# Attention with negated, scaled queries and undivided probabilities, the row sums divided out of a head pair's output

## The chip, the cores and the metric

One Trainium2 chip, one of its NeuronCores. A core has TensorE (PE in the profile, with its weight loads as PEld), VectorE (DVE), ScalarE (ACT), GpSimd (POOL) and SyncE (SP, which here issues nearly all DMAs). Each engine works through its own instructions in order and waits on semaphores for the others. The metric is the device time of one execution in microseconds (us).

## The reference, cut to what matters

The program is one layer of an encoder, applied to two sequences of 512 rows. Beside a recurrent branch (RWKV7, run forwards and backwards) and a feed-forward part it has an attention branch with 8 heads. The change touches this part alone:

```python
sc = (jnp.einsum('bqhd,bkhd->bhqk', qn, k_nope)
      + jnp.einsum('bqhd,bkd->bhqk', qr, k_rope))
prob = jax.nn.softmax(sc.astype(jnp.float32) * scale, axis=-1)   # scale = 96 ** -0.5
return jnp.einsum('bhqk,bkhd->bqhd', prob.astype(v.dtype), v)
```

The softmax of a row is exp(scale * (sc - max)) over its own sum. Dividing by the sum may be done on the probabilities, or on the output row that they are multiplied into.

## The kernel before, in words

The front part of the program (up to about 1000 us) is written as six Python generators, which a small driver (`drive`) interleaves by a virtual clock of TensorE time: each piece of matmul work adds its cost to `pe["now"]`, a generator yields the time at which it wants to go on, and the first one in the list that is due runs next. TensorE instructions are pinned to the order that comes out. The generators, in order of precedence: the recurrence's state steps, its post-processing, the merging of its triangular solves, its preparation, a fill thread (projections, then gates, then the whole attention), and the combination of both branches for the first sequence. The other engines' instructions are placed by a scheduler that simulates the timeline. Constants such as `PL`, `YQ`, `YK` and `YA1` are the virtual times by which the fill thread puts off a step so that its operands may be ready.

Attention goes over 2 sequences, 8 heads and 4 blocks of 128 queries: 64 blocks. For one block:

- `sc`: three fp32r matmuls (high and low parts of queries and keys) of 128x512 into one PSUM bank.
- DVE takes the row maximum into `mx[:, 0:1]` (L605) and multiplies it by -QSCALE (L606).
- ACT computes exp(QSCALE * sc + bias) into `pr` and accumulates the row sum (L608); reading the accumulator is an instruction of its own.
- DVE takes the reciprocal of the sum (L609) and multiplies `pr` by it (L610).
- TensorE transposes `pr` in four pieces into `pt` (L129), and ACT copies `pt` to `pT` (L554). A block waits in the list `pending` until two others stand behind it (`ALAG = 2`), and until `PL` after its scores.

After the fourth block of a pair's second head, `pav` multiplies `pT` of both heads by the values, the even head into partitions 0 to 63 and the odd one into 64 to 127, with queries along the free dimension. DVE copies `pav` to `ob` (L566), which a DMA stores to `o_d`. Queries of the next head come from `attn_q`: six matmuls into `qps`, a multiplication by the rotary table into `qf` on DVE (L539), then a split in high and low parts.

PSUM tiles of the attention (`sc`, `pt`, `pav`, `qps`, `kps`, `vps`) and of the post-processing share four banks (tag "f"), a tile taking the one that comes free; `pr` and `ob` share three buffers in SBUF.

During the attention the recurrence of the last sequences' heads runs in the same stretch (`s`, `o`, `gx`, `gy`, `zp`, `xp` on PE; `rs`, `svb`, `kra`, `bt`, `kt`, `c` on DVE). Towards its end the combination begins: `ld`, `yo` and `pab` on L1032 to L1058, whose loads of `y_d` follow the last post-processing; `pwo` follows at about 1009 us.

Of the kernel before, what the change touches and what calls it, by code (L numbers as in the profile page):

```python
# [10 lines left out]
F32 = mybir.dt.float32  # L11
F32R = mybir.dt.float32r
AF = mybir.ActivationFunctionType
ALU = mybir.AluOpType
AX = mybir.AxisListType
# [3 lines left out]
P = 128  # L19
NB = 2  # L20
S = 512
# [10 lines left out]
QSCALE = 96 ** -0.5  # L32
# [7 lines left out]
ALAG = 2  # L40
# [9 lines left out]
PRE = lambda nc: nc.vector  # L50
# [1 line left out]
NT = 2  # L52
F0 = 10
NE = 2
YA1 = 0.52
YP1 = 7
YP2 = 3
YP3 = 1
# [7 lines left out]
YO2 = 2.11  # L66
YO3 = 3.44
YS = 0.5
YQ = 2.6
YK = 1.4  # L70
OFFS = 200000, 150000, 120000, 100000, 0, 0
JP = NFF // 2
NRH = 10
# [4 lines left out]
HOLDW = 0.7  # L78
PRIOW = 1
C0 = 18  # L80
PL = 3.5
HORD = (0, 1)
VQB = 3
HALVES = (4,)
# [20 lines left out]
def trunk(ctx, tc, outs, x, w_in, w2, g2, w_uq, w_ukk, w_ukv, w_oab, w_out, w_gu, w_down,  # L105
          cols, fng, ident, te, to, mask2, reset, blk64, blk2):
    nc = tc.nc
# [10 lines left out]
    def pin(ins, cost):  # L118
        if pe["pin"]:
            tc.keep_in_program_order(ins)  # L120
        pe["cost"] += cost

    def mm(out, lhsT, rhs, start=True, stop=True, **kw):
        n = math.prod(rhs.shape[1:]) * (1 if rhs.dtype == F32R else 4) / 2400
        pin(nc.tensor.matmul(out, lhsT, rhs, start=start, stop=stop, **kw), n if out.shape[0] > 64 else n / 2)  # L125

    def tr4(ps, src):
        for t in range(4):
            pin(nc.tensor.transpose(ps[:, t * P:(t + 1) * P], src(t), idn), P / 1200)  # L129

    def split(hi, lo, src, eng=None):
        nc.scalar.copy(hi, src)  # L132
        (eng or nc.vector).tensor_sub(lo, src, hi)  # L133

    def mm3(out, whi, wlo, xhi, xlo, start=True, stop=True, **kw):
        mm(out, whi, xhi, start=start, stop=False, **kw)
        yield 0
        mm(out, whi, xlo, start=False, stop=False, **kw)
        yield 0
        mm(out, wlo, xhi, start=False, stop=stop, **kw)  # L140
        yield 0
# [25 lines left out]
    o_d = [[dram.tile([P, S], F32, name=f"o_d{b}{p}") for p in range(NPAIR)] for b in range(NB)]  # L167
# [59 lines left out]
    def pf(name):  # L227
        return psf.tile([P, S], F32, tag="f", bufs=NF, name=name)
# [251 lines left out]
    def attn_ld(ap, src, name, rows=P, q=None):  # L480
        t = ap.tile([P, S], F32, tag="pq", bufs=2, name=name)[0:rows]
        (q or nc.sync).dma_start(t, src)
        return t

    def attn_lat(ap, b, i, t=None):

        if t is None:
            t = attn_ld(ap, mla_d[b][:, i], f"pq{b}{i}", q=None if b else nc.scalar)
        r = [ap.tile([P, S], F32R, tag=f"lat{i}{j}", name=f"lat_{b}{i}{j}") for j in range(2)]
        split(*r, t)  # L490
        return r
# [30 lines left out]
    def attn_kt(kt, ps):  # L522
        for e in range(2):
            rows = slice(0, 64) if e == 0 else slice(64, 128)
            nc.scalar.copy(kt[e][0][rows], ps[rows])
            nc.vector.tensor_sub(kt[e][1][rows], ps[rows], kt[e][0][rows])

    def attn_q(ap, b, hd, qn, tab):
        wq = ap.tile([P, 2 * P], F32, tag="wq", bufs=1, name=f"wq{b}{hd}")
        (nc.sync if b or hd else nc.scalar).dma_start(wq, w_uq[hd])  # L530
        wqh = ap.tile([P, 2 * P], F32R, tag="wqh", bufs=2, name=f"wqh{b}{hd}")
        wql = ap.tile([P, 2 * P], F32R, tag="wql", bufs=2, name=f"wql{b}{hd}")
        split(wqh, wql, wq, QLE(nc))
        ps = pf(f"qps{b}{hd}")
        for i in range(2):
            yield from mm3(ps, wqh[:, i * P:(i + 1) * P], wql[:, i * P:(i + 1) * P], qn[i][0], qn[i][1],
                           start=(i == 0), stop=(i == 1))
        qf = ap.tile([P, S], F32, tag="qf", bufs=1, name=f"qf{b}{hd}")
        nc.vector.tensor_mul(qf, ps, tab[hd % 2])  # L539
        qh = ap.tile([P, S], F32R, tag="qh", bufs=2, name=f"qh{b}{hd}")  # L540
        ql = ap.tile([P, S], F32R, tag="ql", bufs=2, name=f"ql{b}{hd}")
        split(qh, ql, qf, QLE(nc))
        return qh, ql, pe["now"] + pe["cost"] + YQ

    def attention(ap, meanwhile):
        pending = []

        def finish():
            b, hd, qb, pr, pT, at = pending.pop(0)
            p = hd // 2  # L550
            yield "at", at
            pt = pf(f"pt{b}{hd}{qb}")
            tr4(pt, lambda t: pr[:, t * P:(t + 1) * P])
            nc.scalar.copy(pT[hd % 2][:, :, qb * P:(qb + 1) * P], pt.rearrange("p (t q) -> p t q", t=4))  # L554
            if qb < 3 or hd % 2 == 0:
                yield 0
                return
            yield YA1
            pav = pf(f"pav{b}{p}")
            for t in range(4):  # L560
                for e in range(2):
                    mm(pav[e * 64:(e + 1) * 64], vt[b][:, t, (2 * p + e) * 64:(2 * p + e + 1) * 64], pT[e][:, t],
                       start=(t == 0), stop=(t == 3))
                    yield 0
            ob = ap.tile([P, S], F32, tag="pr", bufs=ALAG + 1, name=f"ob{b}{p}")
            nc.vector.tensor_copy(ob, pav)  # L566
            nc.sync.dma_start(o_d[b][p], ob)
            if hd == 7:
                done.add(("attn", b))

        vt = [None] * NB
        pT = [ap.tile([P, 4, S], F32, tag="pT", bufs=2, name=f"pT0{i}") for i in range(2)]
        ldq, ldk = attn_ld(ap, mla_d[0][:, 0], "pq00", q=nc.scalar), attn_ld(ap, mla_d[0][:, 2], "pq02", q=nc.scalar)
        kvn, q0 = attn_lat(ap, 0, 2, ldk), attn_lat(ap, 0, 0, ldq)
        kg = attn_k(ap, 0, 0, kvn)
        meanwhile()
        kps = yield from kg
        qn = [q0, attn_lat(ap, 0, 1)]
        kt = attn_kr(ap, 0)
        attn_kt(kt, kps)  # L580
        tab = []
        for e, src in enumerate((te, to)):
            t = ap.tile([P, S], F32, name=f"tab{e}")
            nc.sync.dma_start(t, src)
            tab.append(t)
        q = yield from attn_q(ap, 0, 0, qn, tab)
        wvr = attn_ld(ap, w_ukv, "wv")
        wv = [ap.tile([P, S], F32R, name=f"wv{j}") for j in range(2)]
        split(*wv, wvr)
        heads = [(b, hd) for b in range(NB) for hd in range(8)]  # L590
        for (b, hd), (b1, hd1) in zip(heads, heads[1:] + [(NB, 0)]):
            qh, ql, at = q
            e = hd % 2
            if e == 0 and (b or hd):
                pT = [ap.tile([P, 4, S], F32, tag="pT", bufs=2, name=f"pT{b}{hd + i}") for i in range(2)]
            if hd == 7 and b1 < NB:
                kvn = attn_lat(ap, b1, 2)
                qn = [attn_lat(ap, b1, i) for i in range(2)]
            for qb in range(4):
                qs = slice(qb * P, (qb + 1) * P)  # L600
                yield "at", at
                sc = pf(f"sc{b}{hd}{qb}")
                yield from mm3(sc, qh[:, qs], ql[:, qs], kt[e][0], kt[e][1])
                mx = ap.tile([P, 4], F32, tag="mx", bufs=4, name=f"mx{b}{hd}{qb}")
                nc.vector.reduce_max(mx[:, 0:1], sc, axis=AX.X)  # L605
                nc.vector.tensor_scalar_mul(mx[:, 1:2], mx[:, 0:1], -QSCALE)  # L606
                pr = ap.tile([P, S], F32, tag="pr", bufs=ALAG + 1, name=f"pr{b}{hd}{qb}")
                nc.scalar.activation(pr, sc, AF.Exp, scale=QSCALE, bias=mx[:, 1:2], accum_out=mx[:, 2:3])  # L608
                nc.vector.reciprocal(mx[:, 3:4], mx[:, 2:3])  # L609
                PRE(nc).tensor_scalar(pr, pr, mx[:, 3:4], 0.0, op0=ALU.mult, op1=ALU.add)  # L610
                pending.append((b, hd, qb, pr, pT, pe["now"] + PL))
                if b1 < NB:
                    if qb == 1:
                        q = yield from attn_q(ap, b1, hd1, qn, tab)
                    if qb == 2 and e == 1:
                        kps = yield from attn_k(ap, b1, hd1 // 2, kvn)
                    if qb == 3 and e == 1:
                        if hd1 == 0:
                            kt = attn_kr(ap, b1)
                        attn_kt(kt, kps)  # L620
                        q = (q[0], q[1], max(q[2], pe["now"] + YK))
                while len(pending) > ALAG:
                    yield from finish()
                if hd == 0 and qb == VQB:
                    vt[b] = yield from attn_v(ap, b, kvn, wv)
        while pending:
            yield from finish()
# [1091 lines left out]
```

## Time and profile before

| | before |
|---|---|
| median of 3 runs | 1831.26 us (1829.73 to 1834.43) |
| time of the profiled execution | 1833.27 us |
| its span, first to last instruction | 1831.4 us |
| PE busy | 1725.9 us, 94% |
| DVE busy | 1116.1 us, 61% |
| ACT busy | 771.4 us, 42% |
| POOL busy | 640.4 us, 35% |
| mean granted TensorE clock | 0.979 |

In views that list instructions, a row has the start in us, the duration in us, the engine, the line and the operation; in brackets stands how long the engine was idle before it, and what ended that. In the views of waits a row has the waiting engine and line, what it waited for, and then the total in us, the number of times and the longest. In tables by stretch each engine has its busy time, with the number of its instructions in brackets; PEclk is the granted TensorE clock. The attention's matmuls start at 721 us with the first `sc`, and the last `pav` ends at 966 us.

### The profile page before, as it was taken

How to read it: one execution, taken by the hardware profiler on the slowest of the kernel's cores; microseconds unless marked ns; L12 is line 12 of the kernel's file. 1: busy time of each engine (PE TensorE's matmuls, PEld its weight loads, DVE VectorE, ACT ScalarE, POOL GpSimd, SP SyncE). 2: the span in 40 equal slices, each digit the busy share in tenths (PEclk: the TensorE clock that was granted, in tenths of full speed). 3: DMA queues.
4: the chain of work that ended last, by engine and by line, in shares of the span. 5: the costliest groups of instructions: out<-in, count | busy, mean ns of one | idle time of the engine just before them, and what ended most of it. 6: DMA issues, size and time to landing. Idle time of an engine off the chain costs nothing.

```text
span 1831.4 us, 30995 instructions
## 1 busy us (share of the span) xinstructions
PE 1725.9 (94%) x11676; PEld 1357.8 (74%) x11676; DVE 1116.1 (61%) x1957; ACT 771.4 (42%) x1496; POOL 640.4 (35%) x992
## 2 busy tenths in 40 slices
PE   6999989999999998899989999699999999989997
PEld 6887767777777775565656979578888888868886
DVE  6633555635355455877776556865655556588757
ACT  5434343333344335666663233333333333335445
POOL 3012345363644627161012124853434333200006
PEclk8999989999999998999999999899999999999999
DMA  4354433434333334212067651022222222374442
GB/s 165 121 175 162 124 106 89 119 80 126 106 107 117 84 109 117 60 34 58 28 240 229 194 175 35 24 81 93 97 96 90 93 81 90 100 270 128 131 139 92
DMA packets 185333, 208.97 MB, mean 114 GB/s; under 512 B 102816, under 2 KB 114464, under 8 KB 185184
## 3 DMA queue, kind: packets, MB, share of 16 engines
q1 hardware_dynamic: 184320, 205.48, 35.9%
q8 instruction: 92, 1.51, 0.3%
q10 hardware_dynamic: 720, 0.98, 0.2%
q0 software_dynamic: 144, 0.52, 0.1%
q14 instruction: 57, 0.47, 0.1%
HBM read 147.70 MB, written 59.24 MB: 113 GB/s over the span
## 4 chain that ended last, share of the span: by engine, by line
PE 67%; DVE 10%; DMA 8%; POOL 7%; issue 4%; ACT 3%; SPq 1%; POOLq 0%; DVEq 0%; ACTq 0%
PE pgC L125 10%; PE pgB L125 6%; PE pgA L125 6%; PE pj_gt L125 6%; PE pj_rkv L125 5%; PE dx L125 5%; PE dy L125 3%; POOL el L841 2%; POOL lt L839 2%; PE pab L125 2%; PE s L125 2%; PE pav L125 2%; PE pj_mla L125 2%; DMA wor<-in_w_out 2%; PE gx L125 2%
## 5 line engine op out<-in xcount | busy, mean ns | idle before, releaser
L839 POOL TENSOR_TENSOR lt<-lane,el 128x126 f32<-128x126 f32 (+22 forms) x248 | 95.6, 386 | 40.8 <-DMA lane<-nt_d 22.3
L841 POOL TENSOR_TENSOR el<-el,lt 128x126 f32<-128x126 f32 (+22 forms) x248 | 98.5, 397 | 19.1
L125 PE MATMUL pab<-yo,wab 128*128 128x512 f32 x384 | 94.8, 400 | 8.3 <-ACT yo L132 3.7
L125 PE MATMUL pj_gt<-h_lo,whi_gt 128*128 128x512 f32 x240 | 99.5, 415 | 0.0
L125 PE MATMUL pj_gt<-h_hi,whi_gt 128*128 128x512 f32 x240 | 99.0, 413 | 0.0
L125 PE MATMUL pj_gt<-h_hi,wlo_gt 128*128 128x512 f32 x240 | 98.4, 410 | 0.5 <-DVE wlo_gt L133 0.5
L125 PE MATMUL pwo<-woh,m 128*128 128x256 f32 x512 | 93.6, 283 | 0.0
L125 PEld LDWEIGHTS pab<-yo,wab 128*128 128x128 f32 x384 | 71.0, 190 | 29.1 <-DVE wab L133 4.8
L1209 POOL TENSOR_TENSOR s<-uraw 128x512 f32<-128x512 f32 x22 | 29.2, 1328 | 153.3 <-DMA uraw<-in_w_gu 153.3
L125 PEld LDWEIGHTS pwo<-woh,m 128*128 128x128 f32 x512 | 80.3, 192 | 0.3
L125 PE MATMUL pj_rkv<-h_hi,whi_rkv 128*128 128x512 f32 x192 | 79.4, 414 | 0.0
L125 PE MATMUL pj_rkv<-h_hi,wlo_rkv 128*128 128x512 f32 x192 | 79.0, 415 | 0.0
L125 PE MATMUL pj_rkv<-h_lo,whi_rkv 128*128 128x512 f32 x192 | 78.4, 409 | 0.0
L125 PE MATMUL pwo<-wol,m 128*128 128x256 f32 x256 | 72.4, 284 | 0.5 <-DVE wol L133 0.5
L1588 POOL TENSOR_TENSOR x<-x,dp 128x512 f32<-128x512 f32 x4 | 6.3, 1590 | 176.9 <-DVE x L1587 176.9
L1277 DVE TENSOR_TENSOR p<-p,pgC 128x512 f32<-128x512 f32 x22 | 15.1, 687 | 86.9 <-PE pgC L125 86.9
L1056 POOL TENSOR_TENSOR g<-g 128x512 f32<-128x512 f32 x16 | 24.5, 1533 | 97.1 <-DVE g L1054 85.9
L928 ACT COPY sva<-s 64x128 f32<-64x128 f32 x64 | 16.5, 257 | 95.6 <-PE s L125 86.3
L466 POOL TENSOR_SCALAR lut<-lut 128x512 f32<-128x512 f32 x32 | 20.5, 642 | 98.4 <-ACT lut L464 98.1
L929 DVE COPY svb<-s 64x128 f32<-64x128 f32 x64 | 18.9, 295 | 57.6 <-ACT sva L928 34.8
L125 PEld LDWEIGHTS pj_gt<-h_hi,wlo_gt 128*128 128x128 f32 x240 | 45.1, 188 | 9.4 <-DVE wlo_gt L133 1.2
L125 PEld LDWEIGHTS pj_gt<-h_hi,whi_gt 128*128 128x128 f32 x240 | 45.1, 188 | 8.8
(1559 smaller groups left out, 5570.2 us busy)
## 6 DMA issues: line engine op xcount, KB each, us to landing
graw<-in_w_gu SPq DMA_DIRECT2D x22, 512.0 KB, 3.5
uraw<-in_w_gu SPq DMA_DIRECT2D x22, 512.0 KB, 3.5
a_d<-a SPq DMA_DIRECT2D x21, 512.0 KB, 3.2
w<-in_w_down SPq DMA_DIRECT2D x42, 256.0 KB, 4.3
x<-in_x SPq DMA_DIRECT2D x16, 512.0 KB, 7.8
rwkv_in<-lut SPq DMA_DIRECT2D x32, 256.0 KB, 2.0
gate_d<-gtt SPq DMA_DIRECT2D x32, 256.0 KB, 2.4
wab<-in_w_oab SPq DMA_DIRECT2D x32, 256.0 KB, 3.5
```

The lines of the kernel that those rows point to most:

```text
L125: pin(nc.tensor.matmul(out, lhsT, rhs, start=start, stop=stop, **kw), n if out.shape[0] > 64 else n / 2)
L466: nc.gpsimd.tensor_scalar(t, t, f, f, op0=ALU.mult, op1=ALU.add)
L839: eng.tensor_mul(lv, lane[:, s, s + 1:].unsqueeze(1).to_broadcast([P, m_, n]), el[:, 0:m_, s].unsqueeze(2).to_broadcast([P, m_, n]))
L841: eng.tensor_add(ev, ev, lv)
L928: nc.scalar.copy(sva[HA, :, c], s2[HA])
L929: nc.vector.tensor_copy(svb[HB, :, c], s2[HB])
L1056: nc.gpsimd.tensor_add(g_[:, 0], g_[:, 0], g_[:, 1])
L1209: vg(ES[min(j, 1)]).tensor_add(s1, a21, a22)
L1277: nc.vector.tensor_add(p1, p1, x_)
L1588: nc.gpsimd.tensor_add(xs(1, t, 1), xs(1, t, 1), p5[t])
```

## The change

1. The queries are multiplied by -QSCALE while they are multiplied by the rotary table (one scalar_tensor_tensor in place of a tensor_tensor, L539). The scores come out negated and scaled.
2. The row minimum of these scores is at once the bias of the exponential, whose scale is -1. The multiplication of `mx` by -QSCALE is gone.
3. The exponential's row sums go into columns of `sm`, a tile of 128x8 for a pair of heads (four query blocks times two heads). `pr` stays undivided: the reciprocal and the multiplication of each block are gone.
4. After the last block of a pair, DVE takes the reciprocal of the 128x8 sums, ACT spreads them to 128x512 (`rb`, each value 64 times), TensorE transposes `rb` in four pieces behind `pav` (`rbp`), ACT copies `rbp` back to `rb`, and DVE multiplies `pav` by it. This multiplication stands where the copy to `ob` stood. `rb` takes the buffer that `ob` had, from before `pav` on.
5. Four virtual times change: `YA1` 0.52 to 0.48, `YQ` 2.6 to 2.18, `YK` 1.4 to 1.63, `PL` 3.5 to 2.81.

```diff
@@ -52,7 +52,7 @@
 NT = 2
 F0 = 10
 NE = 2
-YA1 = 0.52
+YA1 = 0.48
 YP1 = 7
 YP2 = 3
 YP3 = 1
@@ -66,8 +66,8 @@
 YO2 = 2.11
 YO3 = 3.44
 YS = 0.5
-YQ = 2.6
-YK = 1.4
+YQ = 2.18
+YK = 1.63
 OFFS = 200000, 150000, 120000, 100000, 0, 0
 JP = NFF // 2
 NRH = 10
@@ -78,7 +78,7 @@
 HOLDW = 0.7
 PRIOW = 1
 C0 = 18
-PL = 3.5
+PL = 2.81
 HORD = (0, 1)
 VQB = 3
 HALVES = (4,)
@@ -536,14 +536,15 @@
             yield from mm3(ps, wqh[:, i * P:(i + 1) * P], wql[:, i * P:(i + 1) * P], qn[i][0], qn[i][1],
                            start=(i == 0), stop=(i == 1))
         qf = ap.tile([P, S], F32, tag="qf", bufs=1, name=f"qf{b}{hd}")
-        nc.vector.tensor_mul(qf, ps, tab[hd % 2])
+        nc.vector.scalar_tensor_tensor(out=qf, in0=ps, scalar=-QSCALE, in1=tab[hd % 2], op0=ALU.mult, op1=ALU.mult)
         qh = ap.tile([P, S], F32R, tag="qh", bufs=2, name=f"qh{b}{hd}")
         ql = ap.tile([P, S], F32R, tag="ql", bufs=2, name=f"ql{b}{hd}")
         split(qh, ql, qf, QLE(nc))
         return qh, ql, pe["now"] + pe["cost"] + YQ
 
     def attention(ap, meanwhile):
-        pending = []
+
+        pending, sums = [], {}
 
         def finish():
             b, hd, qb, pr, pT, at = pending.pop(0)
@@ -555,6 +556,11 @@
             if qb < 3 or hd % 2 == 0:
                 yield 0
                 return
+            sm = sums.pop((b, p))
+            nc.vector.reciprocal(sm, sm)
+            rb = ap.tile([P, S], F32, tag="pr", bufs=ALAG + 1, name=f"rb{b}{p}")
+            nc.scalar.copy(rb.rearrange("p (t h c) -> p t h c", t=4, h=2),
+                           sm.rearrange("p (t h) -> p t h", t=4).unsqueeze(3).to_broadcast([P, 4, 2, 64]))
             yield YA1
             pav = pf(f"pav{b}{p}")
             for t in range(4):
@@ -562,9 +568,11 @@
                     mm(pav[e * 64:(e + 1) * 64], vt[b][:, t, (2 * p + e) * 64:(2 * p + e + 1) * 64], pT[e][:, t],
                        start=(t == 0), stop=(t == 3))
                     yield 0
-            ob = ap.tile([P, S], F32, tag="pr", bufs=ALAG + 1, name=f"ob{b}{p}")
-            nc.vector.tensor_copy(ob, pav)
-            nc.sync.dma_start(o_d[b][p], ob)
+            ps = pf(f"rbp{b}{p}")
+            tr4(ps, lambda t: rb[:, t * P:(t + 1) * P])
+            nc.scalar.copy(rb, ps)
+            nc.vector.tensor_mul(rb, pav, rb)
+            nc.sync.dma_start(o_d[b][p], rb)
             if hd == 7:
                 done.add(("attn", b))
 
@@ -601,13 +609,13 @@
                 yield "at", at
                 sc = pf(f"sc{b}{hd}{qb}")
                 yield from mm3(sc, qh[:, qs], ql[:, qs], kt[e][0], kt[e][1])
-                mx = ap.tile([P, 4], F32, tag="mx", bufs=4, name=f"mx{b}{hd}{qb}")
-                nc.vector.reduce_max(mx[:, 0:1], sc, axis=AX.X)
-                nc.vector.tensor_scalar_mul(mx[:, 1:2], mx[:, 0:1], -QSCALE)
+                if e == qb == 0:
+                    sums[b, hd // 2] = ap.tile([P, 8], F32, tag="sm", bufs=2, name=f"sm{b}{hd}")
+                sm = sums[b, hd // 2]
+                mx = ap.tile([P, 1], F32, tag="mx", bufs=4, name=f"mx{b}{hd}{qb}")
+                nc.vector.tensor_reduce(mx, sc, axis=AX.X, op=ALU.min)
                 pr = ap.tile([P, S], F32, tag="pr", bufs=ALAG + 1, name=f"pr{b}{hd}{qb}")
-                nc.scalar.activation(pr, sc, AF.Exp, scale=QSCALE, bias=mx[:, 1:2], accum_out=mx[:, 2:3])
-                nc.vector.reciprocal(mx[:, 3:4], mx[:, 2:3])
-                PRE(nc).tensor_scalar(pr, pr, mx[:, 3:4], 0.0, op0=ALU.mult, op1=ALU.add)
+                nc.scalar.activation(pr, sc, AF.Exp, scale=-1.0, bias=mx, accum_out=sm[:, qb * 2 + e:qb * 2 + e + 1])
                 pending.append((b, hd, qb, pr, pT, pe["now"] + PL))
                 if b1 < NB:
                     if qb == 1:
```

The instructions move on all engines, only in this stretch and in the loads just behind it. Three places follow.

DVE, in the stretch in which the recurrence's preparation (`bt`, `kt`, `kra`, the scan `c`, the sums `os`) stands between the parts of the softmax; before, from the scaling of one block's maximum to the division of the same block:

```order
L606 TENSOR_SCALAR mx_8264<-mx_8264 128x1
L526 TENSOR_TENSOR kt_7896<-kps_8240,kt_7895 64x512
L864 STREAM_TRANSPOSE tp_8447<-e_8446 128x256
L871 COPY z_8292<-zp_8298 32x256
L605 TENSOR_REDUCE mx_8332<-sc_8315 128x1
L961 TENSOR_TENSOR os_8145<-os_8145,rbp_gn_8324 128x512
L758 TENSOR_TENSOR kra_8426<-nkk_8283,pp_8394 128x8x64
L759 TENSOR_TENSOR kra_8426<-rkv_8006,pp_8394 128x8x64
L609 RECIPROCAL mx_8264<-mx_8264 128x1
L741 TENSOR_TENSOR bt_8398<-bt_8398,c_8389 128x512
```

Seven rows further on stands the division `pr_8267<-pr_8267,mx_8264` (L610), behind four more of the preparation's operations, a maximum and the scaling of another. With the change the same place reads:

```order
L560 RECIPROCAL sm_8014<-sm_8014 128x8
L616 TENSOR_REDUCE mx_8297<-sc_8266 128x1
L872 STREAM_TRANSPOSE tp_8427<-e_8426 128x256
L879 COPY z_8273<-zp_8279 32x256
L748 SCALAR_TENSOR_TENSOR bt_8402<-nkk_8260,a_8395 128x512
L616 TENSOR_REDUCE mx_8324<-sc_8307 128x1
L969 TENSOR_TENSOR os_8141<-os_8141,rbp_gn_8316 128x512
L766 TENSOR_TENSOR kra_8414<-nkk_8260,pp_8382 128x8x64
```

Of a block's softmax only the row minimum is left among the preparation's operations, and one reciprocal for the pair.

PE, at the end of the first pair of heads, before (`pt_8438` is the transposition of the pair's last block, `zp` and `xp` belong to the merging):

```order
L125 MATMUL qps_8362<-lat_7887,wql_8359 128x512
L129 MATMUL pt_8438<-idn,pr_8267 128x128 x4
L125 MATMUL zp_8455<-tp_8447,ntl_8448 32x32 x16
L125 MATMUL pav_8472<-pT_7855,vt_8128 64x512
L125 MATMUL pav_8472<-pT_7856,vt_8128 64x512
```

and with the change, from the same transposition on:

```order
L129 MATMUL pt_8347<-idn,pr_8246 128x128 x4
L125 MATMUL xp_8358<-e_8270,z_8273 32x32 x16
L125 MATMUL pav_8419<-pT_7855,vt_8117 64x512
L125 MATMUL pav_8419<-pT_7856,vt_8117 64x512
L125 MATMUL pav_8419<-pT_7855,vt_8117 64x512
L125 MATMUL pav_8419<-pT_7856,vt_8117 64x512
L125 MATMUL zp_8435<-tp_8427,ntl_8428 32x32 x16
L125 MATMUL pav_8419<-pT_7855,vt_8117 64x512
L125 MATMUL pav_8419<-pT_7856,vt_8117 64x512
L125 MATMUL pav_8419<-pT_7855,vt_8117 64x512
L125 MATMUL pav_8419<-pT_7856,vt_8117 64x512
L129 MATMUL rbp_8456<-idn,rb_8354 128x128 x4
```

The transposition keeps its place behind the query projection, the merging's matmuls sit elsewhere, and four transpositions follow `pav`.

DVE at the end of the sixth pair, late in the attention, where only a few other operations remain, before:

```order
L566 COPY ob_10559<-pav_10550 128x512
L605 TENSOR_REDUCE mx_10566<-sc_10562 128x1
L606 TENSOR_SCALAR mx_10566<-mx_10566 128x1
L605 TENSOR_REDUCE mx_10583<-sc_10579 128x1
L609 RECIPROCAL mx_10566<-mx_10566 128x1
L606 TENSOR_SCALAR mx_10583<-mx_10583 128x1
L610 TENSOR_SCALAR pr_10569<-pr_10569,mx_10566 128x512
L605 TENSOR_REDUCE mx_10600<-sc_10596 128x1
```

Between one maximum and the next stand a scaling, a reciprocal and a division. With the change, from the first row minimum of the next head on:

```order
L616 TENSOR_REDUCE mx_10471<-sc_10467 128x1
L574 TENSOR_TENSOR rb_10363<-pav_10450,rb_10363 128x512
L616 TENSOR_REDUCE mx_10485<-sc_10481 128x1
L616 TENSOR_REDUCE mx_10499<-sc_10495 128x1
L616 TENSOR_REDUCE mx_10513<-sc_10509 128x1
```

The operation that reads `pav` now stands behind the first row minimum of the next head, and the row minima of the blocks follow each other.

## The prediction

> **What bounds the kernel now.** I read the page first, then the table by stretch, then the waits of PE in the stretch that the change touches. The chain of work that ended last, by engine:
>
> ```profile
> PE 67%; DVE 10%; DMA 8%; POOL 7%; issue 4%; ACT 3%; SPq 1%; POOLq 0%; DVEq 0%; ACTq 0%
> ```
>
> PE leads, but every tenth microsecond of the chain is DVE's. The table by stretch (length, then busy us and instructions of PE, PEld, DVE, ACT, POOL, then clock, DMA share, GB/s), for the attention, its last part, its most crowded 20 us, and one late pair of heads:
>
> ```profile
> 721.00:966.00 245.00, 222.15 (x1894) 147.87 (x1892) 188.77 (x473) 148.16 (x341) 60.74 (x125) 0.97 0.27 84
> 913.00:966.00 53.00, 44.52 (x201) 27.23 (x200) 41.22 (x94) 30.93 (x68) 6.78 (x5) 0.94 0.65 224
> 740.00:760.00 20.00, 13.99 (x133) 9.86 (x133) 18.86 (x40) 14.56 (x30) 4.94 (x7) 0.95 0.25 79
> 919.40:938.60 19.20, 18.01 (x88) 12.06 (x88) 15.96 (x41) 14.22 (x32) 0.00 (x0) 1.00 0.87 321
> ```
>
> The reader is to see two regimes. Over the whole attention PE is idle for 245.0 - 222.2 = 22.8 us: it is the bound, with gaps. In 740 to 760 DVE is busy for 94% and PE for 70%: there DVE is the bound. What ended PE's gaps, from the view of waits for 721 to 966:
>
> ```profile
> PE pt L129 <- DVE pr L610: 6.5, 6, 3.9
> PE pab L125 <- ACT yo L132: 3.7, 1, 3.7
> PE pt L129 <- ACT pT L554: 2.2, 3, 1.4
> PE s L125 <- DVE svb L929: 1.8, 3, 0.8
> PE sc L125 <- DVE kt L509: 1.5, 1, 1.5
> PE pt L129 <- DVE kt L526: 1.2, 1, 1.2
> PE pav L125 <- ACT pT L554: 1.1, 2, 0.8
> PE vps L125 <- ACT pT L554: 0.8, 1, 0.8
> ```
>
> The largest single wait, 3.9 us, is a transposition that waits for the division of its block. The timeline of DVE shows why, and the timeline of PE what it costs:
>
> ```profile
> 754.01 0.15 DVE L609 RECIPROCAL mx<-mx 128x1 f32<-128x1 f32 x1
> ...
> 757.14 1.22 DVE L734 TENSOR_TENSOR_SCAN c<-rst,c 128x512 f32<-128x512 f32 x1
> 758.27 0.46 DVE L610 TENSOR_SCALAR pr<-pr,mx 128x512 f32<-128x512 f32 x1
> ```
>
> ```profile
> 758.79 1.12 PE L129 MATMUL pt<-idn,pr 128*128 128x128 f32 x4 [3.93 <-DVE pr L610]
> ```
>
> The reciprocal was done at 754.2, the division began at 758.3: it needed nothing but its turn, behind the recurrence's operations and a scan of 1.22 us. The clock falls with that wait. Two stretches right behind the two longest waits, and the chain through `pav` in the first and elsewhere:
>
> ```profile
> 758.00:764.90 6.90, 6.11 (x46) 2.89 (x48) 6.74 (x16) 4.43 (x8) 0.96 (x3) 0.51 0.07 19
> ...
> 956.00:962.80 6.80, 5.19 (x14) 3.08 (x16) 4.56 (x7) 2.42 (x4) 0.61 (x2) 0.50 0.47 154
> ```
>
> ```profile
> 760.90 5.52 PE pav L125 x14
> ```
>
> ```profile
> 932.45 1.38 PE qps L125 x6
> ...
> 934.26 4.32 PE pav L125 x16
> ```
>
> At half clock 14 pieces of `pav` took 5.52 us; at 0.27 us apiece, as in the 16 at full clock, they would take 3.8.
>
> **What goes.** The grouped view of the same stretch has the operations (count, busy us, mean ns, then idle time before them and its causes):
>
> ```profile
> L608 ACT ACTIVATE pr<-sc,mx 128x512 f32<-128x512 f32 x64 | 44.0, 688 | 13.8 <-DVE mx L606 10.9 <-PE pt L129 1.3 <-DVE rs L909 1.1
> ...
> L554 ACT COPY pT<-pt 128x512 f32<-128x512 f32 x64 | 37.3, 583 | 27.9 <-PE pt L129 27.4
> L610 DVE TENSOR_SCALAR pr<-pr,mx 128x512 f32<-128x512 f32 x64 | 32.5, 511 | 0.8
> ...
> L539 DVE TENSOR_TENSOR qf<-qps,tab 128x512 f32<-128x512 f32 x15 | 10.3, 689 | 1.4 <-PE qps L125 1.0
> L609 DVE RECIPROCAL mx<-mx 128x1 f32<-128x1 f32 x64 | 10.0, 156 | 6.1 <-ACT pr L608 5.5
> ...
> L606 DVE TENSOR_SCALAR mx<-mx 128x1 f32<-128x1 f32 x64 | 9.4, 147 | 0.6
> ```
>
> Per block L606, L609 and L610 leave DVE: 147 + 156 + 511 = 814 ns, 52 us over 64 blocks, 28% of the 188.8 that DVE works here. That is not time on the path. What counts is that a block passes DVE once instead of four times, so that PE's waits on this queue shrink:
>
> - The division is gone, and with it the 6.5 us (between 3.9, the one understood wait, and 6.5). What is late next is the exponential itself, which needs the row minimum's turn on DVE. I take 6.5.
> - If that 3.9 us wait is gone, the half clock behind it goes too: 5.52 - 3.8 = 1.7 us on `pav` and some on the pieces before it. I take 2.2; the ends are 0 and half of 6.9, 3.4.
> - Waits on `pT`, 2.2 + 1.1 + 0.8 = 4.1: these copies stand on ACT behind exponentials that waited 10.9 us for L606. Three quarters, 3.1 (0 to 4.1).
> - Waits on `kt`, 1.5 + 1.2 = 2.7, DVE's queue again; three quarters, 2.0 (0 to 2.7).
> - Waits on `svb`, 1.8: half, 1.0 with rounding (0 to 1.8), since ACT and POOL take part in them.
>
> Sum: 6.5 + 2.2 + 3.1 + 2.0 + 1.0 = 14.8 (3.9 to 18.5).
>
> **What comes.** Four more transpositions, one more ACT pair and a changed DVE operation at each of 8 pairs. Nearest rows: transpositions in a row of PE's timeline, the spreading copy and the multiplication that the post-processing already does, the present copy of `pav`, and a scalar_tensor_tensor out of PSUM:
>
> ```profile
> 920.45 0.71 PE L125 MATMUL sc<-kt,qh 128*128 128x512 f32 x2
> ...
> 921.23 0.60 PE L129 MATMUL pt<-idn,pr 128*128 128x128 f32 x4
> 921.59 0.71 PE L125 MATMUL sc<-kt,qh 128*128 128x512 f32 x2
> ```
>
> ```profile
> L186 ACT COPY rb_gn<-gnr x3: 617/617/618, 745.3 to 906.7; 128x512 f32<-128x512 f32 x3
> ```
>
> ```profile
> L961 DVE TENSOR_TENSOR os<-os,rbp_gn x8: 678/687/689, 344.4 to 911.1; 128x512 f32<-128x512 f32 x8
> ```
>
> ```profile
> L566 DVE COPY ob<-pav x8: 691/692/693, 768.1 to 965.9; 128x512 f32<-128x512 f32 x8
> ```
>
> ```profile
> L718 DVE SCALAR_TENSOR_TENSOR nkk<-kk,rbp_kk x8: 673/682/689, 164.3 to 745.0; 128x512 f32<-128x512 f32 x8
> ```
>
> - Four transpositions hold PE from 921.23 to 921.59, 0.36 us; 8 times, 2.9 us, straight on the path.
> - On DVE a multiplication (687 ns) replaces a copy (692), and 16 fused multiplications (682) replace 16 plain ones (689): nothing. The 8 reciprocals, at the 156 ns of a 128x1 one or some more, make 1.3 us in DVE's new room.
> - ACT gets 8 x (617 + 583) ns = 9.6 us on 148 of 245; PE's work hides it as long as no copy that PE waits for stands behind it. Without that cover it is 9.6.
> - The new wait: the multiplication must await `rbp` and its copy, so the two banks of `pav` and `rbp` come free late. Behind the last `pav`, PE has `rbp` (0.36), a score block (921.23 - 920.45 = 0.78 in the same timeline) and a transposition (0.36), 1.5 us, before it needs one of them. `rbp`'s bank is free after 0.36 + 0.58 and three hand-overs of about 0.1, 1.2 us: no wait if ACT is free. `pav`'s is free another 0.8 later, at 2.0. I take 0.2 us a pair, 1.6 (0 to 1.3 a pair, 10.4, if ACT and DVE each have one more 128x512 operation, 0.6 to 0.7 us, ahead). Queued behind this multiplication on DVE are the next row minima and the recurrence's `bt` and `kt`.
> - At the end of the attention PE waits 3.7 us for `yo`, whose chain comes from the loads:
>
> ```profile
> 949.94 3.79 DMA ld<-y_d
> ...
> 955.18 1.74 DVE ld L1038
> ...
> 956.94 0.63 ACT yo L132
> ```
>
> PE arrives there earlier, the loads not quite as much: part of what is won behind 913 is given back. I take 1.0. The end is 4.8, all of PE's other idle time there (53.0 - 44.5 - 3.7).
>
> Sum: 2.9 + 1.6 + 1.0 = 5.5 (2.9 to 18.1). Net: 14.8 - 5.5 = 9.3 us less. The profiled execution took 1833.27 us, 1.9 about its span of 1831.4 and 2.0 above the median; 1833.3 - 9.3 = 1824.0 on its scale, **1822 us** against the median of 1831.26. Behind 966 us the order on PE is the same, and the loads of `pwo`'s weights start with the attention's end, so I carry the shift through.
>
> [...] The row first: the second halved stretch, 956.0 to 962.8, also stands behind a wait of more than 3.5 us, and none behind the waits of 1.5 us and less. [...]
>
> The other row: one division took 1.42 us instead of 0.46 while POOL worked.
>
> ```profile
> 943.74 2.70 POOL L1037 TENSOR_TENSOR ld<-ld,bg 128x512 f32<-128x512 f32 x2 [37.09 <-DMA ld<-y_d]
> ```
>
> ```profile
> 943.88 1.42 DVE L610 TENSOR_SCALAR pr<-pr,mx 128x512 f32<-128x512 f32 x1
> ```
>
> [...]
>
> **The rivals.**
>
> *More than that, 1816 us.* All terms at their good ends: 18.5 - 2.9 = 15.6. For it: the late pair takes 19.2 us, and its work, 24 score matmuls at 0.26, 15 projections at 0.23 (six `qps` took 1.38 in the chain of waits), 8 transpositions at 0.36 and `pav` at 4.3, makes 16.9; short waits hide in what counts as busy. Against: ACT and the switching between kinds of matmul stay.
>
> *Hidden, 1829 us.* The 4.8 us behind 913 are all given back, and the bank wait is 0.6 a pair, 4.8: the gain is 14.8 - 2.9 - 4.8 - 4.8 = 2.3. For it: the loads before `yo`, with 0.65 of the DMA engines busy. Against: the long waits lie before 913.
>
> *Slower, 1839 us.* The way from `pav` to the freed bank, PE to ACT to DVE instead of DVE alone, stops PE at each pair. It decides from the point at which each of the two steps finds one more 128x512 operation ahead: 10.4 + 2.9 + 1.0 = 14.3 come, and as the long queue on DVE and the clock then stay, only the 6.5 of the division go: 7.8 more. For it: ACT is busy for 14.2 of 19.2 us in the late pair. Against: DVE loses 28% of its work, and PE has 1.5 us to cover 1.2.
>
> **How the numbers follow.** Forecast 0.48, more 0.15, hidden 0.25, slower 0.12. About 0.3% (5.5 us, below 1825.8 or above 1836.8) is what a measurement can tell from no change. Faster: 0.42 of the forecast's 0.48, all 0.15, and 0.03 of the hidden case, 0.60. Slower: 0.11 and 0.02, 0.13. The rest, 0.27, is no change. The range goes from 1813, a little below the best ends, to 1834, past the hidden case; what is left out is most of the slower case and a little below. The forecast's own range is 1816 to 1828.
>
> **What would show it.** Right: DVE busy for about 138 us between the first `sc` and the last `pav` (188.8 - 52 + 1), no PE wait above 1.5 us at the first pair's end and no halved clock behind it, and the span from first `sc` to last `pav` near 236 us. `rbp` should show 32 transpositions at 8 places, 0.36 us each place. Wrong: PE waits at `sc` or `pt` behind each `rbp` for ACT or DVE `rb` of 0.6 us or more; a wait for `yo` that has grown by what the attention won; or a `pt` that waits as long for the exponential as it did for the division.

## The result, and the profile after

The changed kernel takes 1814.53 us (median of 5 runs, 1812.06 to 1816.27) against 1831.26 (five runs as well, 1829.73 to 1834.43): a ratio of 0.9903, 95% interval 0.9889 to 0.9916, 16.7 us less. Run a second time, beside three of the experiments (as e5), it came to 0.9927 (0.9909 to 0.9945), 13 us less. The forecast was 1822, the range 1813 to 1834.

The last `pav` turned out to be a poor mark for the end of the attention, since the moved order also puts pieces of `pab` behind it that stood ahead of it before. A better stretch goes from the first score matmul to the first matmul of the output projection, `pwo`: by then PE has done the same work in all the kernels here to within two matmuls, the 32 transpositions of `rbp` apart. The table by stretch (start and end, length, then busy us and instructions of PE, PEld, DVE, ACT, POOL, then clock, DMA share, GB/s) for it, before:

```profile
721.10:1008.70 287.60, 261.76 (x2059) 178.53 (x2058) 216.69 (x512) 163.56 (x366) 70.02 (x131) 0.97 0.34 107
```

and after, with the 20 us that were the most crowded before:

```profile
717.30:991.30 274.00, 260.34 (x2093) 183.13 (x2091) 177.34 (x327) 169.74 (x382) 70.37 (x131) 0.98 0.36 112
740.00:760.00 20.00, 19.27 (x238) 12.33 (x238) 19.63 (x33) 15.93 (x32) 4.60 (x6) 1.00 0.27 90
```

The stretch is 287.6 - 274.0 = 13.6 us shorter, of which 12.2 are PE's idle time (25.8 to 13.7). DVE has lost 39 us of busy time: 64 x 814 ns are 52, but in these traces its operations overlap at their ends. Added up one by one they take 50 us less (238 to 188), and busy time counts an overlap once. In 740 to 760 it is even fuller than before, 19.6 of 20 us against 18.9, but PE is now busy there for 19.3 us instead of 14.0. The other 4.7 of the 18.3 us between the two profiles lie outside: 3.8 before the first score (721.1 against 717.3), where the order of every engine is the same, and 0.9 behind the first `pwo` (1831.4 - 1008.7 = 822.7 against 1813.1 - 991.3 = 821.8). In the profiles of the experiments the first score starts anywhere from 715.2 to 720.5, so the 3.8 is scatter of single executions and no effect of the change.

PE's waits after the change, in the same stretch (us in total, times, longest):

```profile
PE pab L125 <- ACT yo L132: 2.5, 1, 2.5
PE pt L129 <- ACT pr L618: 1.7, 4, 0.7
PE s L125 <- DVE rs L917: 1.5, 3, 0.8
PE pab L125 <- DVE wab L133: 1.3, 2, 0.9
PE pab L125 <- ACT wab L132: 1.0, 1, 1.0
PE pt L129 <- ACT pT L555: 1.0, 2, 0.8
PE sc L125 <- DVE kt L509: 0.9, 1, 0.9
PE s L125 <- DVE svb L937: 0.9, 3, 0.4
```

The line that led before, `pt` for the division with 6.5 us, has no successor of that size: the exponential that a transposition now waits for costs 1.7 in all and 0.7 at the longest. `yo` leads, and it is 1.2 us shorter than it was. Two waits have grown: for `rs` from 0.6 to 1.5, and for `wab`, the weights of the combination, from 1.1 to 2.3. What the change added shows in the view of `rbp` and `rb`:

```profile
L129 PE MATMUL rbp<-idn,rb x32: 272/273/329, 753.0 to 939.3; 128*128 128x128 f32 x32
L562 ACT COPY rb<-sm x8: 620/621/627, 748.5 to 933.7; 128x512 f32<-128x512 f32 x8
L573 ACT COPY rb<-rbp x8: 580/586/587, 753.7 to 942.5; 128x512 f32<-128x512 f32 x8
L574 DVE TENSOR_TENSOR rb<-pav,rb x8: 680/688/692, 756.8 to 943.3; 128x512 f32<-128x512 f32 x8
```

### The profile page after: what moved, and what is told of

Same layout as the page of the kernel before. It is cut to its first block, busy times and chain, and to the rows that moved or that the text cites. A ratio compares the mean times of both kernels' runs of the same rounds, so it can differ in the third digit from the quotient of the medians.

```text
span 1813.1 us, 30886 instructions
## 1 busy us (share of the span) xinstructions
PE 1719.7 (95%) x11708; PEld 1359.8 (75%) x11708; DVE 1074.9 (59%) x1773; ACT 778.1 (43%) x1512; POOL 641.4 (35%) x992
## 4 chain that ended last, share of the span: by engine, by line
PE 66%; DVE 10%; DMA 9%; POOL 7%; issue 4%; ACT 3%; SPq 1%; DVEq 0%; POOLq 0%; ACTq 0%
PE pgC L125 10%; PE pgB L125 6%; PE pj_gt L125 6%; PE pgA L125 6%; PE dx L125 5%; PE pj_rkv L125 5%; PE dy L125 3%; POOL lt L847 2%; POOL el L849 2%; PE s L125 2%; PE pab L125 2%; PE pj_mla L125 2%; DMA wor<-in_w_out 2%; PE pwo L125 2%; PE gx L125 2%
## 5 line engine op out<-in xcount | busy, mean ns | idle before, releaser
L466 POOL TENSOR_SCALAR lut<-lut 128x512 f32<-128x512 f32 x32 | 20.2, 634 | 98.7 <-ACT lut L464 98.3
L616 DVE TENSOR_REDUCE mx<-sc 128x1 f32<-128x512 f32 x64 | 43.8, 688 | 18.5 <-PE sc L125 17.9
```

The lines of the kernel that those rows point to most:

```text
L466: nc.gpsimd.tensor_scalar(t, t, f, f, op0=ALU.mult, op1=ALU.add)
L616: nc.vector.tensor_reduce(mx, sc, axis=AX.X, op=ALU.min)
```

## The experiments

Three theories were tried against each other. QUEUE: PE's gaps come from how much work stands in DVE's queue. CHAIN: they come from the division's place in a block's own way from exponential to transposition. ORDER: the gain comes from the four constants that set where PE's pieces stand, and so from another order. A fourth, STANDING, comes in with e7: DVE's queue is held up because DVE stands and waits for the exponential. All ratios are against the kernel before, run alternately on the same chip.

### The operations without the order, and the order without the operations

e1 is the changed kernel with the old constants, e4 the kernel before with the new ones:

```diff
-YA1, YQ, YK, PL = 0.48, 2.18, 1.63, 2.81   # e1
+YA1, YQ, YK, PL = 0.52, 2.6, 1.4, 3.5
```

```diff
-YA1, YQ, YK, PL = 0.52, 2.6, 1.4, 3.5      # e4
+YA1, YQ, YK, PL = 0.48, 2.18, 1.63, 2.81
```

> The changed kernel with the four constants of the kernel before (0.52, 2.6, 1.4, 3.5), so that PE's pieces are ordered by the old times. Theories: QUEUE, the gain comes from DVE's lighter queue, and CHAIN, it comes from the shorter way of a block from its score to its transposition: both expect most of the 16.7 us, 1815 to 1819 us. ORDER, the gain comes from where the new constants put the pieces on PE: about 1831 us, and the changed constants alone give the rest.

> The kernel before with the four constants of the change. ORDER: about 1817 us. QUEUE and CHAIN: no gain, 1831, or slower, up to 1836, because a transposition is then placed 0.7 earlier behind its score block while its division is as late as before, so the waits of PE for the division grow above 6.5 us.

e1: 1823.11 us, ratio 0.9961 (0.9946 to 0.9977), 7.1 us less (4.2 to 9.9). e4: 1825.84, ratio 0.9975 (0.9959 to 0.9991), 4.6 us less (1.6 to 7.5). No theory was right alone, and all three missed both times: the operations give some 7 us and the order some 5, and their sum, 11.7, agrees with the 13 and 17 of the whole within the intervals. What the order adds on top of the new operations, e1 against the changed kernel, is 6 to 11 us. The waits say what each does. e1's stretch from first score to first `pwo`, and PE's waits in it:

```profile
717.90:997.20 279.30, 261.03 (x2091) 179.25 (x2090) 177.00 (x327) 169.66 (x382) 69.96 (x131) 0.99 0.35 110
```

```profile
PE s L125 <- DVE svb L937: 2.2, 2, 1.3
PE pav L125 <- ACT pT L555: 2.1, 3, 1.1
PE pab L125 <- ACT wab L132: 2.1, 2, 1.9
PE qps L125 <- ACT pT L555: 1.8, 2, 1.5
PE sc L125 <- DVE kt L509: 1.4, 1, 1.4
```

and in e4's:

```profile
717.70:997.50 279.80, 256.04 (x2059) 176.78 (x2058) 214.88 (x511) 162.32 (x366) 70.37 (x131) 0.98 0.35 110
```

```profile
PE pt L129 <- DVE pr L610: 9.5, 6, 5.0
PE pab L125 <- ACT wab L132: 3.7, 2, 2.8
...
PE s L125 <- DVE svb L929: 1.4, 3, 0.8
...
PE sc L125 <- DVE kt L509: 0.9, 1, 0.9
...
PE pt L129 <- ACT pT L554: 0.3, 1, 0.3
```

The two stretches are 8.3 and 7.8 us shorter than before. These are single executions: e4's has 826.7 us behind the stretch, where the kernel before had 822.7 with the same order, so the timed 7.1 and 4.6 are the better figures.

With the old order the wait for the division is gone, and the waits for the copies `pT` stay (5.1 in all, against 4.6 in the same stretch before). With the new order alone it is the other way round: 0.3 of the waits for `pT` is left, and the wait for the division grows from 6.5 to 9.5 us, as expected of a transposition placed earlier behind a division that is as late as ever. Only both together remove both.

### One half of the operations at a time

e2 is the kernel before with negated, scaled queries and the minimum as bias, each block still divided. e3 keeps the maximum and its scaling, and divides a pair's output. Both have the old constants.

```diff
-nc.vector.reduce_max(mx[:, 0:1], sc, axis=AX.X)                          # e2
-nc.vector.tensor_scalar_mul(mx[:, 1:2], mx[:, 0:1], -QSCALE)
-nc.scalar.activation(pr, sc, AF.Exp, scale=QSCALE, bias=mx[:, 1:2], accum_out=mx[:, 2:3])
+nc.vector.tensor_reduce(mx[:, 0:1], sc, axis=AX.X, op=ALU.min)
+nc.scalar.activation(pr, sc, AF.Exp, scale=-1.0, bias=mx[:, 0:1], accum_out=mx[:, 2:3])
...                              # and the queries times -QSCALE, as in the change
```

```diff
-nc.vector.tensor_reduce(mx, sc, axis=AX.X, op=ALU.min)                   # e3, from e1
+nc.vector.reduce_max(mx[:, 0:1], sc, axis=AX.X)
+nc.vector.tensor_scalar_mul(mx[:, 1:2], mx[:, 0:1], -QSCALE)
...                              # and the queries, the exponential and mx as before
```

> The kernel before with negated, scaled queries and the row's minimum as the bias, but each block still divided on DVE. It removes one DVE operation of 147 ns a block, 9.4 of the 52 us that the whole change takes from DVE. QUEUE, in proportion: 16.7 x 9.4 / 52 = 3.0 us less, 1828. CHAIN: 147 ns less of way and the division still in it, 1829 to 1831. Either way the clock still halves behind a wait of over 3 us for a division.

> The changed kernel's undivided probabilities and its division of a pair's output, with the old maximum, its scaling on DVE and the old constants. Removes 667 of the 814 ns a block on DVE. QUEUE, in proportion: 13.7 us less than before, 1817 to 1819. CHAIN: all of what the changed kernel has with the old constants, within 1 us. ORDER: about 1831.

e2: 1828.21 us, ratio 0.9986 (0.9975 to 0.9998), 2.6 us less (0.4 to 4.6) for 9.4 us of DVE's work. That is near QUEUE's 3.0, but CHAIN's 0 to 2 lies in the interval too, so e2 tells little. e3: 1826.24, ratio 0.9979 (0.9967 to 0.9990), 3.8 less for 42.7 us of DVE's work, far from the 13.7 that QUEUE had in proportion. That figure was taken from the 16.7 us of the whole, the order's share included; in proportion to e1's 7.1 it would be 5.8, just within e3's interval (1.8 to 6.0). The two halves add up to 6.4, e1's 7.1 within the intervals.

### DVE's load put back without the division

e6, e7 and e12 put work on DVE behind each exponential of the changed kernel, for which nothing on another engine waits: a ballast. In e6 and e7 it is two reciprocals of one column and a multiplication of the queries' table by one, in place; only DVE reads this table. In e12 it is one reciprocal alone, of the block's sum.

```diff
+nc.vector.reciprocal(scm[:, 0:1], scm[:, 1:2])                           # e6, e7; scm holds ones
+nc.vector.reciprocal(scm[:, 0:1], scm[:, 1:2])                           # e6; e7 and e12 read the block's sum in sm
+nc.vector.tensor_scalar(tab[0], tab[0], scm[:, 1:2], 0.0, op0=ALU.mult, op1=ALU.add)   # e6, e7
```

> The changed kernel again, as the base of the three beside it. All theories: 0.9903 of the kernel before, as it was, within 0.0025; the stretch from the first score matmul to the first of the output projection (pwo) 274 us, with 13 to 14 us of PE idle.

> The changed kernel with the DVE work of each block put back as idle ballast: behind each exponential two 128x1 reciprocals and one 128x512 multiplication by 1.0 of the query table in place, about 0.8 us, which wait for nothing and for which no block waits. QUEUE (PE's gaps come from DVE's load): the gain falls back to that of the new order alone, 1823 to 1827 us, idle of PE 20 us or more. CHAIN (they come from the division standing between the exponential and the transposition): 1814 to 1818 us.

> The same ballast, but the second reciprocal reads the block's sum, so that DVE stands and waits for the exponential as it did before; still no block waits for the ballast. CHAIN: 1814 to 1818 us. QUEUE: 1823 to 1828. A third theory, STANDING (what costs is DVE's queue held up behind each exponential, not its work): this kernel is slower than the ballast without the wait by 3 us or more, with PE waiting for row minima, kt and svb.

> The changed kernel with one 128x1 reciprocal of the block's sum (156 ns) behind each exponential on DVE, written to a spare column, for which nothing waits: DVE stands for the exponential as before, with only 10 us of work put back. QUEUE, by the ballast without a wait, which put 46 us on DVE for 15 us: 10 x 15 / 46 = 3.3 us more than the changed kernel, 1816 to 1819. STANDING, by the difference of the two ballasts (7.8): 3.3 + 7.8 = 11 more, 1823 to 1828. CHAIN: no difference, 1813 to 1816.

e5 (the changed kernel): 1814.15 us. e6: 1829.44, ratio 1.0004 (0.9992 to 1.0016). e7: 1837.21, ratio 1.0048 (1.0030 to 1.0066). e12: 1818.64, ratio 0.9945 (0.9931 to 0.9958). e6 is the verdict on CHAIN: no block waits for this work, the probabilities are undivided, the order is the new one, and the whole gain is gone. QUEUE's own range, 1823 to 1827, was missed as well: e6 is slower than e4 (0.9975), which has the same constants and a DVE as busy (214.9 us), by some 5 us, the intervals just apart. The amount of DVE's work doesn't explain these, and what does isn't shown. Its ballast by DVE's groups (count, busy us, mean ns, idle before; part of the short records is missing), its stretch and its waits:

```profile
L623 DVE TENSOR_SCALAR tab<-tab,scm 128x512 f32<-128x512 f32 x62 | 30.5, 491 | 0.6
```

```profile
715.20:1003.90 288.70, 264.04 (x2092) 182.22 (x2091) 213.94 (x488) 170.25 (x381) 68.83 (x130) 0.98 0.34 106
```

```profile
PE s L125 <- DVE rs L922: 3.6, 3, 2.3
PE s L125 <- DVE svb L942: 2.6, 4, 1.0
PE pab L125 <- DVE g L1067: 2.2, 1, 2.2
PE sc L125 <- DVE kt L509: 2.2, 1, 2.2
```

DVE is back at 213.9 us and the stretch at 288.7, where the kernel before had 216.7 and 287.6. The waits are another set: not the transposition now, but the recurrence's `rs` and `svb` and the next keys `kt`, which stand behind the ballast. Here, what is late depends on what is queued, and that something is late on the load.

STANDING got half an answer. e7 is 7.8 us slower than e6, as that theory wants. But e12, whose reciprocal made DVE stand for 6.2 us in all with 10 us of work,

```profile
L621 DVE RECIPROCAL scm<-sm 128x1 f32<-128x1 f32 x64 | 10.0, 156 | 6.8 <-ACT pr L620 6.2
```

is 3.3 us slower than e5 by the ratios (4.5 by the medians), and their intervals overlap. That is QUEUE's 3.3 and far from STANDING's 11, but no proof of either: the stretches of e5 and of e12,

```profile
715.90:988.90 273.00, 257.54 (x2091) 181.67 (x2091) 177.56 (x327) 169.34 (x382) 68.86 (x131) 0.99 0.36 112
```

```profile
715.90:989.90 274.00, 259.22 (x2092) 183.04 (x2090) 183.25 (x392) 169.78 (x383) 70.67 (x131) 0.98 0.35 112
```

differ by 1.0 us, and the rest lies behind them. By itself, then, standing costs little; on a full queue it seems to cost more. Where e7's time goes beside e6 its profile doesn't settle. Its stretch is 3.2 us longer (291.9), with PE idle for less of it (22.0 us against 24.7) but at a lower clock (0.95 against 0.98), and the rest lies in the unchanged parts ahead and behind.

### The division on POOL

e9 is the kernel before with the multiplication of a block by its reciprocal on the other engine:

```diff
-PRE = lambda nc: nc.vector
+PRE = lambda nc: nc.gpsimd
```

> The kernel before, old order, with each block's 128x512 multiplication by the reciprocal on POOL instead of DVE; minimum, scaling and reciprocal stay on DVE. DVE loses 32.5 of its 188.8 us in the attention, while the block's way from exponential to transposition gets longer, since the nearest POOL operation of 128x512 took about 1.3 us where DVE takes 0.5. QUEUE: faster than before, in proportion to the 7.1 us that the change gave with the old order 32.5 / 52 x 7.1 = 4.4 us, 1825 to 1828 us if the longer way costs nothing. CHAIN: slower than before, each late block by some of the 0.8 us more, 1832 to 1845. STANDING: little change, since DVE still stands behind each exponential for the reciprocal.

e9: 1824.81 us, ratio 0.9983 (0.9970 to 0.9997), 3.1 us less (0.5 to 5.5). The division got longer and PE waits for it longer than before:

```profile
L610 POOL TENSOR_SCALAR pr<-pr,mx x64: 689/696/1659, 723.8 to 948.1; 128x512 f32<-128x512 f32 x64
```

```profile
PE pt L129 <- POOL pr L610: 7.9, 8, 2.0
```

696 ns for 486 (median), 7.9 us of waits for 6.5, and yet the kernel is faster: CHAIN falls a second time, and QUEUE's 4.4 is within the interval. STANDING's little change isn't excluded, as the interval begins at 0.5. The waits are eight of at most 2.0 us in place of one of 3.9 and some short ones.

### What the added work costs, and two ways onward

e8 leaves out the division altogether; e10 gives the combination behind the attention three buffers where it has two; e11 moves the subtractions for the low halves of queries and their weights from DVE to POOL.

```diff
-nc.vector.reciprocal(sm, sm)                  # e8
...                                            # and the spreading copy into rb
-ps = pf(f"rbp{b}{p}")
-tr4(ps, lambda t: rb[:, t * P:(t + 1) * P])
-nc.scalar.copy(rb, ps)
-nc.vector.tensor_mul(rb, pav, rb)
+nc.vector.tensor_copy(rb, pav)
```

```diff
-tag="ld", bufs=2                              # e10; the same for both tiles of tag g3
+tag="ld", bufs=3
```

```diff
-split(qh, ql, qf, QLE(nc))                    # e11; the same for wqh, wql
+split(qh, ql, qf, nc.gpsimd)
```

> The changed kernel without the division at all: sums not inverted, spread, transposed or multiplied in, and the output of a pair copied by DVE as in the kernel before. The attention's output is left undivided. It prices what the change adds: forecast 2.9 us of transpositions and 1.6 us of waits for a bank, so 1810 us where the changed kernel takes 1814.5; if only the transpositions count, 1811.6; if the way from pav to the freed bank stops PE at each pair (the rival), 1801 to 1805.

> The changed kernel with three buffers in place of two for the tiles that the combination behind the attention loads (ld and the tiles of gate and bonus). If the 2.5 us wait for yo and the halved clock behind it come from loads that stand in the queue for a buffer: the wait goes below 1 us, no halved clock at 942 to 951, and 3 to 7 us less than the changed kernel, 1808 to 1812. If they come from the transfers themselves (DMA engines busy for 0.8 to 1.0 of 948 to 960) or from the combination's own operations: within 2 us of it, 1813 to 1816.

> The changed kernel with the low halves of the queries and of their weights (16 subtractions of 128x512 and 14 of 128x256, 17.5 us on DVE in the attention) on POOL, which is busy for 58 of 222 us there. QUEUE: another 17.5 / 52 of the 16.7 us at most, 0 to 5 us less than the changed kernel, since only 8 us of PE idle are left in the attention: 1810 to 1815. CHAIN (a longer way to the scores, 1.3 for 0.7 us at each head): PE waits at sc for ql grow by up to 0.6 us a head, 1815 to 1824.

e8: 1814.93 us, ratio 0.9927 (0.9910 to 0.9943), the same as e5 beside it. Its stretch is shorter than e5's 273.0 by 5.3 us:

```profile
717.60:985.30 267.70, 253.92 (x2060) 179.17 (x2059) 175.57 (x319) 161.38 (x366) 69.24 (x131) 0.98 0.36 115
```

but its profile has 825.4 us behind the stretch and e5's 822.0, and the timed runs show nothing of the 5.3. So the added work costs at most some 5 us, and why leaving it out brings nothing at the end stays open. The rival by which the way from `pav` to the freed bank stops PE at each pair (10 us and more) is out.

e10: 1812.65 us, ratio 0.9904 (0.9891 to 0.9918). The wait for `yo` is gone, and another has come in its place, for weights whose load was issued at 948.2 and landed at 957.4:

```profile
PE pab L125 <- ACT wab L132: 3.0, 1, 3.0
```

The stretch is 269.2, some 4 us shorter, but the ratio lies between the two that the changed kernel had (0.9903 and 0.9927): no gain that these runs can tell. A third buffer removes the wait for `yo`, but two are not its whole cause: in e1 and e4, with two, it is 0.6 and 0.7, with longer waits for `wab` in its place. e11: 1818.13, ratio 0.9940 (0.9926 to 0.9954). That is not faster, and whether it is slower is open: it is slower than the 0.9903 of the changed kernel's first runs, but its interval overlaps that of e5's 0.9927. The time lies in CHAIN's range, yet the waits for `ql` that CHAIN asked for don't appear. Its stretch, 274.1, is as long as the changed kernel's, and its waits on DVE are no shorter in sum: with 13.7 us of idle left there was little for QUEUE to win. Nothing here clearly beats the changed kernel.

## Why the prediction was right, and where it was not

The direction, the main cause and the range held; the forecast's 9.3 us were too few beside 13 to 17, because one source of the gain had no term. Step by step:

- **The division's wait, 6.5, and the halved clock behind it, 2.2**: right. The wait is gone, the longest for an exponential in its place is 0.7, and no halved clock stands behind the first pair (the granted clock is full from 719.6 to 941.4). From the first score to the first `pav` the changed kernel needs 30.6 us, where it needed 39.7 (`pav`'s first rows at 747.9 and 760.8).
- **The reason given, DVE's queue and not the division's length**: right, and shown by e6 and e9. The sharper claim that a block passes DVE once instead of four times was not what counted: unrelated work in the same queue brought the whole loss back. How much the queue's work is worth is known only roughly: e6 lost more than its amount explains.
- **The waits on `pT`, 3.1 of 4.1**: right in amount (1.0 is left), wrong in cause. They were put to exponentials on ACT that waited 10.9 us for the scaling on DVE. The views of ACT's waits, e1's and then e4's, have

```profile
ACT pr L618 <- DVE mx L616: 13.5, 19, 2.0
```

```profile
ACT pr L608 <- DVE mx L606: 10.9, 16, 2.1
```

In e1 the scaling is gone, but the exponentials wait even longer for the row minimum, and PE's waits for `pT` are as long as before. In e4 the exponentials wait as they did, and PE's waits for `pT` are nearly gone. The order took them.
- **That is the step that failed**: the four constants. The text showed the moved rows but gave the order no price; every gain stood for DVE's relief. By e4 the order alone is worth 4.6 us. The forecast's 9.3 is within e1's interval, 4.2 to 9.9, but that is luck in part: it counts the 3.1 for `pT`, which the operations alone don't bring.
- **The waits on `kt` and `svb`, 2.0 and 1.0**: 1.8 and 0.9 less, right in amount. The reason is again only half right: with the operations alone (e1) the wait of 1.2 for `kt` at L526 goes, but the one for `kt` at L509 stays at 1.4 and that for `svb` is 2.2; with the order alone (e4) they are 0.9 and 1.4.
- **The new wait for a bank, 1.6**: nothing. At the first pair `rbp` ran at 752.97, its copy at 753.72, and the multiplication stood in DVE's full queue until 756.76. It ended at 757.44, 4.4 us behind the last `pav`, where the forecast had 2.0 and a cover of 1.5. Still none of PE's waits names it: the next score blocks began at 755.32 and 757.67. The cover was counted from attention pieces alone and left out the recurrence's, such as `xp`, that stand between.

```profile
752.97 0.66 PE L129 MATMUL rbp<-idn,rb 128*128 128x128 f32 x4
753.38 0.70 PE L125 MATMUL sc<-kt,qh 128*128 128x512 f32 x2
...
754.16 0.60 PE L129 MATMUL pt<-idn,pr 128*128 128x128 f32 x4
754.69 0.69 PE L125 MATMUL xp<-e,z 32*32 32x32 f32 x32
755.32 0.73 PE L125 MATMUL sc<-kt,qh 128*128 128x512 f32 x2
```

```profile
756.76 0.68 DVE L574 TENSOR_TENSOR rb<-pav,rb 128x512 f32<-128x512 f32 x1
```

- **Given back at `yo`, 1.0**: that wait got shorter, 3.7 to 2.5. What was given back stands elsewhere, in the waits for `rs` and `wab` (0.9 and 1.2 more), for which the sum had no term. The first loads of `y_d` stand on SP behind a store of the attention's output; they were issued at 924.9, 16 us earlier than before (940.8).
- **The mark "first score to last `pav` near 236"**: 221.7, far off, in part because 7 pieces of `pab` moved behind that mark. DVE was busy for 142.9 us up to it, where 138 were forecast.
- **The rivals**: "more than that", 1816, came nearest in time, and its cheap end of what is added held; the rest of its reasons were not it, since what it lacked was the order. "Hidden" and "slower" fell: the wait for `yo` gave nothing back, and no wait of PE names the bank.

## What to carry to other kernels

When an engine that is not the bound is full in one stretch, price a change by how much work it takes out of that engine's queue there, and expect the waits to move to whatever is queued next. That gives an order of size and no price: a microsecond of DVE's work was worth from 0.1 us (3.8 for 42.7 in e3, 3.1 for 32.5 in e9) to 0.3 us here (14 for 46 in e6, beside e5). When a change comes with new numbers for the order, cost them as an edit of their own, by a kernel that has them alone: here they were worth 4.6 us by themselves, about a third of the gain, and they removed another wait than the operations did. And take as the mark for a stretch a point by which the same instructions have run in both kernels.

## What the runs showed of the hardware

The halved clock did not go by the length of a wait alone. In the changed kernel's first profile PE waited 2.53 us for `yo` and ran at half clock behind it for 10.2 us; in its second (e5) the same wait was 2.36 us and the clock stayed. PE's rows of the two:

```profile
942.08 3.23 PE L125 MATMUL pab<-yo,wab 128*128 128x512 f32 x6 [2.53 <-ACT yo L132]
```

```profile
940.46 0.50 PE L125 MATMUL pab<-yo,wab 128*128 128x512 f32 x1 [2.36 <-ACT yo L132]
```

In all the traces here the granted clock changes on a fixed raster: two changes in one execution lie a multiple of 3.4133 us apart, to within a few ns (2 ns for the 25 changes in the trace before and the 19 in the first trace after). The tables by stretch, cut at the steps of this raster, of the first profile and then of the second:

```profile
938.02:941.43 3.41, 1.52 (x8) 0.47 (x5) 1.79 (x2) 0.02 (x1) 2.48 (x2) 1.00 0.07 25
941.43:944.85 3.42, 2.77 (x6) 1.78 (x6) 2.44 (x4) 1.69 (x3) 0.00 (x0) 0.50 0.71 230
...
948.26:951.67 3.41, 3.41 (x10) 2.64 (x9) 1.00 (x2) 1.26 (x3) 0.00 (x0) 0.50 0.89 268
```

```profile
936.32:939.73 3.41, 1.78 (x9) 0.56 (x5) 1.71 (x2) 0.00 (x0) 2.48 (x2) 1.00 0.13 50
939.73:943.14 3.41, 1.93 (x6) 1.05 (x6) 2.52 (x5) 2.32 (x4) 0.00 (x0) 1.00 0.62 211
```

The first wait puts 1.89 us of PE's idle time into one step (3.41 - 1.52), and the next step is halved; the clock stays so until a step without idle time (948.26 to 951.67) has passed, and is full again from 951.67. The second wait is split by a step's end, 1.63 us in one and, with the short waits behind it, 1.48 in the next, and nothing is halved. From 700 to 998 us of all fourteen profiles, each of the 37 steps at full clock with more than 1.70 us of idle time was followed by a halved one, of the 65 with 1.0 to 1.70 only 6 were, and of those with less none. What decides between 1.0 and 1.70 isn't known; PE's busy time is modelled and some records are missing, so these figures are rough. In the first profiles of the two kernels alone, the 6 steps with 1.89 to 3.08 us were each followed by a halved one, and the 6 with 1.05 to 1.70 by none. In the kernel before, the 3.7 us wait for `yo` put 2.02 us of idle time into the step ahead of the halved one (952.51 to 955.92). In the changed kernel that wait was shorter, 2.53 and 2.36 us, and the clock halved behind it in one execution and not in the other, which fits with where the wait fell on the raster.

The other surprise is POOL's multiplication of a 128x512 block by a number per partition, 696 ns (median) where an operation on two such tiles took it about 1.3 us (1288 ns, median, for `ld` at L1037 in the profile before): the expectation for e9 had its price twice too high. A nearer row stood in the profile before: POOL's multiplication and addition of constants on a 128x512 tile (`lut`, L466) took 620 ns (median).
